# Gated convolution layer: three of four pairs of projection tiles computed by seven half-size products

## The chip, the cores and the metric

One core of a Trainium2 chip runs the kernel. The time is the device time of one execution in microseconds (us). TensorE (PE in the profile) multiplies matrices and has a row of its own for weight loads (PEld); VectorE (DVE), ScalarE (ACT) and GpSimd (POOL) work on tiles in the on-chip memory SBUF; the first two also read PSUM, where TensorE writes its sums. SyncE (SP) issues the transfers. Each engine has a queue of its own, filled in the order of the program.

## The reference

One inference step of a 4-layer decoder trunk on 512 prompt positions and 8 samples, 520 columns in all, with a model width of 1024. The layers have different mixers (matrix memory, short gated convolution, dilated attention, pooling). The change is in the second, the convolution:

```
u = h @ w_in                                  # 520x1024 @ 1024x8192
bg, cg, xb, z = split(u, 4)                   # each 2048 wide
cx = cg * xb
y  = w0 * cx[t-2] + w1 * cx[t-1] + w2 * cx[t] # three taps, per channel
out = (bg * y * silu(z)) @ w_out              # 2048x1024
```

Here h is rms_norm(x) times a gain. Everything is float32.

## The kernel before, in words

Activations lie transposed, 128 channels on the partitions and 520 columns. A float32 product is made of three products of a reduced format (float32r): each operand is split into a high part (a copy to float32r by ScalarE) and a low part (operand minus high part, by VectorE), and high x high, high x low and low x high are added up in PSUM. `mm6` (lines 193 to 203) does this for one 128x128 block of weights and all 520 columns: six matmuls, of 256 and 264 columns by turns. `proj` (213 to 225) makes one output tile of 128 channels from eight such blocks, 48 matmuls, into one of two PSUM buffers, and after every second block lets background streams take a step (`tick`).

The convolution (`conv`, 782 to 819) runs over 16 tiles of 128 channels. For tile j it projects xb, cg, bg and z (weight tiles 32+j, 16+j, j and 48+j of `w_b`), multiplies cg by xb (line 799), applies the taps (ScalarE line 807, VectorE lines 810 to 813), multiplies by bg (814) and by silu(z), and splits the result y into high and low part for the output projection (`gated`, 516 to 533).

The order of work is written out by hand. `plan` lists all weight tiles in the order of use. `weights` (181) keeps three weight tiles ahead split by `cast` (169: ScalarE line 175, VectorE line 177) and more ahead loaded by `fetch` (161), on SyncE's queue. At the start of a layer `finish_norm` (300 to 342) finishes the norm of the input behind the first projections: the mean square by a matmul (line 313), square root, reciprocal (316), then, one block of channels after the other, the normalised input (329) and its high and low parts (330, 333). Until that is done the projections use the raw input, and VectorE multiplies what comes out of PSUM by the reciprocal (`scaled`, 266 to 283). The output projection makes its first two tiles together (`proj_pair`, 227 to 241) and asks for y blocks as it needs them (`need`, 243 to 248).

Of the kernel before, what the change touches and what calls it, by code (L numbers as in the profile page):

```python
# [8 lines left out]
F32 = mybir.dt.float32  # L9
F32R = mybir.dt.float32r  # L10
# [25 lines left out]
NCOL = 120  # L36


def plan():

    out = []

    def end(i, name, halves, begun=False):
        cs = range(2 if halves else 1)
        out.extend((name, j, c) if halves else (name, j) for c in cs for j in range(2) if c or not begun)
        out.extend((name, j, c) if halves else (name, j) for j in range(2, KD) for c in cs)
        for j in range(KD):
            if j % 4 == 0:
                out.append(("w_pe", i, j // 4))
            out.append(("w_pg", i, j))  # L50

    for hd in range(H):
        out.extend(("w_a", j) for j in (hd, 8 + hd, 16 + 2 * hd, 17 + 2 * hd, 32 + 2 * hd, 33 + 2 * hd))
    out.extend(("w_a", 48 + j) for j in range(16))
    end(0, "w_ao", True)
    for j in range(16):
        out.extend(("w_b", 16 * q + j) for q in (2, 1, 0, 3))
    end(1, "w_bo", True)
    for hd in range(H):
        out.extend(("w_c", 8 * q + hd) for q in range(9))  # L60
    out.extend(("w_c", 72 + j) for j in range(H))
    end(2, "w_co", False)
    for g in range(4):
        for n, (u, i) in enumerate(POOLED):
            if g and n == 2:
                out.extend(("w_grp", g - 1, i) for i in range(2))
            out.append(("w_d", 16 * u + 4 * g + i))
    out.extend(("w_do", j, 0) for j in range(2))
    out.extend(("w_grp", 3, i) for i in range(2))
    end(3, "w_do", True, True)  # L70
    return out


class Stream:
# [39 lines left out]
class Net:  # L114
    def __init__(self, ctx, tc, d):
        self.tc, self.nc, self.d = tc, tc.nc, d
        nc = self.nc
        ctx.enter_context(tc.manual_schedule())
        pool = lambda name, **kw: ctx.enter_context(tc.tile_pool(name=name, **kw))
        self.cp = pool("const", bufs=1)  # L120
        self.wp = pool("w", bufs=3)
# [7 lines left out]
        self.gate, self.finish = Gate(0.5), None  # L129
        self.wkeys, self.wf, self.wc = plan(), {}, {}  # L130
        self.wpos = self.ndma = self.ncast = 0
# [26 lines left out]
        return self.cols[:, i : i + 1]  # L158


    def fetch(self, upto):
        while self.ndma < min(upto, len(self.wkeys)):
            key = self.wkeys[self.ndma]
            wf = self.wp.tile([P, 1024], F32, tag="wf", name=self.nm("wf"))
            self.nc.sync.dma_start(wf, self.d[key[0]][key[1:]])
            self.wf[self.ndma] = wf
            self.ndma += 1

    def cast(self, upto):
        nc = self.nc  # L170
        while self.ncast < min(upto, len(self.wkeys)):
            self.fetch(self.ncast + 1)
            wf = self.wf.pop(self.ncast)
            wh = self.wp.tile([P, 1024], F32R, tag="wh", name=self.nm("wh"), bufs=4)
            nc.scalar.activation(wh, wf, AF.Copy)  # L175
            wl = self.wp.tile([P, 1024], F32R, tag="wl", name=self.nm("wl"), bufs=4)
            nc.vector.tensor_sub(wl, wf, wh.bitcast(F32))  # L177
            self.wc[self.ncast] = (wh, wl)
            self.ncast += 1

    def weights(self, *key, ahead=4):
        i = self.wpos
        assert self.wkeys[i] == key, (self.wkeys[i], key)
        self.wpos += 1
        self.cast(i + ahead)
        self.fetch(i + 2 + ahead)
        return self.wc.pop(i)

    def tick(self):
        for s in self.streams:  # L190
# [2 lines left out]
    def mm6(self, ps, w, c, a, start, stop, m=P):  # L193

        mm = self.nc.tensor.matmul
        wh, wl = w[0][:, c : c + m], w[1][:, c : c + m]
        out = [self.part(ps, j, m) for j in range(2)]
        for j in range(2):
            mm(out[j], wh, a[0][:, PARTS[j]], start=start, stop=False)  # L199
        for j in range(2):  # L200
            mm(out[j], wh, a[1][:, PARTS[j]], start=False, stop=False)  # L201
        for j in range(2):
            mm(out[j], wl, a[0][:, PARTS[j]], start=False, stop=stop)  # L203

    @staticmethod
    def part(ps, j, m=P):
# [6 lines left out]
    def proj(self, name, *idx, a):  # L213

        ps = self.psum()
        n = len(a)
        if a is self.h:
            self.raw, a = self.hraw, list(a)
        for c in range(0, n, 8):
            w = self.weights(name, *idx, *([c // 8] if n > 8 else []))  # L220
            for k in range(8):
                self.mm6(ps, w, k * P, a[c + k], c + k == 0, c + k == n - 1)
                if k % 2:
                    self.tick()
        return ps[:, BASE : BASE + T]

    def proj_pair(self, name, a, n):

        ps = self.psum(), self.psum()
        for c in range(0, n, 8):  # L230
            w = []
            for lo, hi in ((0, 7), (7, 8)) if c + 8 == n else ((0, 8),):
                for j in range(2):
                    if not lo:
                        w.append(self.weights(name, j, *([c // 8] if n > 8 else []), ahead=4 - j))
# [6 lines left out]

    def need(self, a, i):

        while len(a) <= i:
            if not (self.gate.gens or self.gate.run):
                self.finish()
            self.gate.step()
# [51 lines left out]
    def finish_norm(self, hs, g0, wait, idle, pace):  # L300

        nc = self.nc
        self.r = self.act()
# [3 lines left out]
        def work():  # L307
# [13 lines left out]
                return  # L321
            for _ in range(idle):
                yield
            new = []
            for k in range(KD):
                for _ in range(pace):
# [14 lines left out]
        self.norm = Stream(1)  # L341
        self.norm.gens.append(work())


    def out_proj(self, name, y, i, begun=None):

# [6 lines left out]
        for j in range(KD):  # L353
# [4 lines left out]
            ps = pair[j] if j < 2 else self.proj(name, j, a=y)  # L358
            nc.vector.tensor_add(self.x[j], ps, self.x[j])  # L359
            xs.append(self.split(self.x[j]))  # L360
        return xs

    def embed(self, i, xs):
# [4 lines left out]
        for j in range(KD):  # L368
# [19 lines left out]
        self.finish_norm(hs, g0, 3, *((4, 4), (2, 3), (0, 0))[i])  # L388
        return hs

    def final(self, xs, pe, xg):
# [390 lines left out]
    def conv(self, h, lay):  # L782
        nc, d, tc = self.nc, self.d, self.tc
        self.streams = [self.norm, self.gate]
        y = []
        ex = lay.enter_context(tc.tile_pool(name="cvy", bufs=16))
        with ExitStack() as st:
            mp = st.enter_context(tc.tile_pool(name="cv", bufs=1))
            sin = mp.tile([P, 16, 2, NS], F32, name="cv_in")
# [4 lines left out]
            for j in range(16):  # L794
# [8 lines left out]
                nc.gpsimd.tensor_copy(po[:, j], cx[:, NP - 2 : NP])  # L803
                nc.gpsimd.tensor_copy(so[:, j, 1], cx[:, NP:T])
                w0, w1, w2 = (self.col(C_CW + 16 * t + j) for t in range(3))
                yc = self.act()
                nc.scalar.activation(yc, cx, AF.Copy, scale=w2)
                ps = self.proj("w_b", j, a=h)
                stt = nc.vector.scalar_tensor_tensor
                stt(yc[:, 1:NP], cx[:, 0 : NP - 1], w1, yc[:, 1:NP], ALU.mult, ALU.add)  # L810
                stt(yc[:, 2:NP], cx[:, 0 : NP - 2], w0, yc[:, 2:NP], ALU.mult, ALU.add)
                stt(yc[:, NP:T], sin[:, j, 1], w1, yc[:, NP:T], ALU.mult, ALU.add)
                stt(yc[:, NP:T], sin[:, j, 0], w0, yc[:, NP:T], ALU.mult, ALU.add)
                nc.vector.tensor_mul(yc, self.ready(ps), yc)
                z = self.scaled(self.proj("w_b", 48 + j, a=h), func=AF.Silu)
                self.gated(y, z, yc, True, pools=(None, ex))
            nc.sync.dma_start(d["o_conv_p"], po)
            nc.sync.dma_start(d["o_conv_s"], so)
        return y
# [519 lines left out]
```

## Time and profile before

| | us |
|---|---|
| median of 3 runs (1 core) | 2192.27 |
| lowest and highest run | 2191.33 and 2192.53 |
| the profiled execution, its own time | 2191.75 |
| its span, first to last instruction | 2190.0 |
| TensorE busy in the span | 2170.4 (99%) |
| mean granted TensorE clock | 0.999 of full speed |

The page of the profile gives the busy time of each engine, the chain of work that ended last (followed back from the last instruction), and groups of instructions by line and shape. The trace behind it can be asked for a stretch, a line or the order of time. A matmul's shown duration contains its way through the array, which overlaps the next one, so the pace of matmuls is read from the distance of their starts or from counts over a stretch.

### The profile page before, as it was taken

How to read it: one execution, taken by the hardware profiler on the slowest of the kernel's cores; microseconds unless marked ns; L12 is line 12 of the kernel's file. 1: busy time of each engine (PE TensorE's matmuls, PEld its weight loads, DVE VectorE, ACT ScalarE, POOL GpSimd, SP SyncE). 2: the span in 40 equal slices, each digit the busy share in tenths (PEclk: the TensorE clock that was granted, in tenths of full speed). 3: DMA queues.
4: the chain of work that ended last, by engine and by line, in shares of the span. 5: the costliest groups of instructions: out<-in, count | busy, mean ns of one | idle time of the engine just before them, and what ended most of it. 6: DMA issues, size and time to landing. Idle time of an engine off the chain costs nothing.

```text
span 2190.0 us, 42581 instructions
## 1 busy us (share of the span) xinstructions
PE 2170.4 (99%) x17788; PEld 2154.2 (98%) x17788; DVE 1336.6 (61%) x2984; ACT 784.0 (36%) x1286; POOL 226.8 (10%) x338
## 2 busy tenths in 40 slices
PE   9999999999999999999999999999999999999998
PEld 8999999999999999999999999999999999999998
DVE  7677676653575344333467877787777466676434
ACT  6444444432442222222333323333335343222233
POOL 1101110100000000000014232232220000000000
PEclk9999999999999999999999999999999999999999
DMA  4643544333232322233233645554545233323421
GB/s 151 203 163 139 184 168 150 98 97 97 90 97 87 97 89 95 92 105 95 83 103 127 187 168 179 172 181 155 184 161 194 87 106 97 97 88 97 124 88 51
DMA packets 104643, 275.17 MB, mean 126 GB/s; under 512 B 33316, under 2 KB 37668, under 8 KB 102404
## 3 DMA queue, kind: packets, MB, share of 16 engines
q1 hardware_dynamic: 104308, 272.41, 38.3%
q8 instruction: 139, 2.28, 0.4%
q14 instruction: 52, 0.43, 0.1%
q10 hardware_dynamic: 144, 0.06, 0.0%
HBM read 249.61 MB, written 22.82 MB: 124 GB/s over the span
## 4 chain that ended last, share of the span: by engine, by line
PE 91%; DVE 3%; ACT 1%; POOL 1%; issue 0%; DMA 0%; SPq 0%; POOLq 0%; DVEq 0%; ACTq 0%
PE ps L199 27%; PE ps L201 27%; PE ps L203 27%; PE ax L925 1%; PE ax L998 1%; PE ax L201 1%; PE ax L203 1%; PE ax L199 1%; PE ax L969 1%; PE ax L654 1%; PE ax L673 1%; DVE wl L177 1%; DVE a L329 0%; POOL a L877 0%; PE ax L936 0%
## 5 line engine op out<-in xcount | busy, mean ns | idle before, releaser
L199 PE MATMUL ps<-hi,wh 128*128 128x256 f32 (+1 forms) x5280 | 1086.3, 287 | 2.1 <-DVE a L278 1.6
L201 PE MATMUL ps<-lo,wh 128*128 128x256 f32 (+1 forms) x5280 | 1062.9, 283 | 0.1
L203 PE MATMUL ps<-hi,wl 128*128 128x256 f32 (+1 forms) x5280 | 1063.1, 283 | 0.0
L199 PEld LDWEIGHTS ps<-hi,wh 128*128 128x128 f32 x5280 | 822.3, 189 | 7.6 <-issue 2.5
L201 PEld LDWEIGHTS ps<-lo,wh 128*128 128x128 f32 x5280 | 819.3, 188 | 0.3 <-DVE lo L530 0.3
L203 PEld LDWEIGHTS ps<-hi,wl 128*128 128x128 f32 x5280 | 818.3, 188 | 0.0
L177 DVE TENSOR_TENSOR wl<-wf,wh 128x1024 fp32r<-128x1024 f32 x344 | 429.2, 1249 | 397.1 <-ACT wh L175 395.5
L175 ACT ACTIVATE wh<-wf 128x1024 fp32r<-128x1024 f32 x344 | 361.0, 1051 | 253.2 <-issue 201.7
L271 ACT ACTIVATE a<-ps 128x520 f32<-128x520 f32 x94 | 56.3, 599 | 247.7 <-PE ps L203 243.5
L876 POOL TENSOR_TENSOR a<-a,a 32x520 f32<-32x520 f32 x48 | 74.0, 1542 | 386.2 <-DVE a L278 199.6
L359 DVE TENSOR_TENSOR x<-ps,x 128x520 f32<-128x520 f32 x32 | 22.4, 699 | 103.4 <-PE ps L203 103.3
L278 DVE TENSOR_TENSOR a<-ps,a 128x520 f32<-128x520 f32 x95 | 65.9, 694 | 25.9 <-PE ps L203 22.5
L282 ACT ACTIVATE a<-a 128x520 f32<-128x520 f32 x43 | 27.5, 639 | 150.2 <-DVE a L278 150.0
L259 ACT ACTIVATE hi<-x 128x520 fp32r<-128x520 f32 x32 | 20.5, 639 | 164.6 <-DVE x L359 164.6
L877 POOL TENSOR_TENSOR a<-a,a 32x520 f32<-32x520 f32 x48 | 66.4, 1384 | 124.8 <-DVE a L875 88.7
L902 ACT ACTIVATE S<-S,nmx 128x128 f32<-128x128 f32 (+1 forms) x96 | 40.0, 417 | 76.1 <-DVE nmx L899 76.1
L252 DVE CUSTOM_DVE_ANT_0 kc<-kc,qb 128x128 f32<-128x128 f32 (+1 forms) x192 | 56.8, 350 | 12.5 <-DMA kc<-kc 12.5
L252 DVE CUSTOM_DVE_ANT_0 vc<-vc,pb 128x128 f32<-128x128 f32 (+1 forms) x192 | 61.6, 379 | 0.0
L880 DVE TENSOR_TENSOR a<-a,a 32x520 f32<-32x520 f32 x48 | 37.2, 776 | 17.3 <-POOL a L877 17.3
L260 DVE TENSOR_TENSOR lo<-a,hi 128x520 fp32r<-128x520 f32 x40 | 28.0, 699 | 31.3 <-ACT hi L259 31.3
L732 DVE SCALAR_TENSOR_TENSOR Ci<-kqb,wv,Ci 128x128 f32<-128x128 f32 x128 | 37.1, 346 | 12.2 <-DMA kqb<-scr_kq 10.1
L528 ACT ACTIVATE hi<-a 128x520 fp32r<-128x520 f32 x40 | 25.4, 635 | 50.6 <-DVE a L525 50.6
(272 smaller groups left out, 1759.7 us busy)
## 6 DMA issues: line engine op xcount, KB each, us to landing
wf<-w_c SPq DMA_DIRECT2D x80, 512.0 KB
wf<-w_a SPq DMA_DIRECT2D x64, 512.0 KB
wf<-w_b SPq DMA_DIRECT2D x64, 512.0 KB
wf<-w_pg SPq DMA_DIRECT2D x32, 512.0 KB
wf<-w_d SPq DMA_DIRECT2D x32, 512.0 KB
pb<-scr_p SPq DMA_DIRECT2D x8, 1292.0 KB
Ci<-C_in SPq DMA_DIRECT2D x16, 512.0 KB
kqb<-scr_kq SPq DMA_DIRECT2D x8, 1024.0 KB
```

The lines of the kernel that those rows point to most:

```text
L175: nc.scalar.activation(wh, wf, AF.Copy)
L177: nc.vector.tensor_sub(wl, wf, wh.bitcast(F32))
L199: mm(out[j], wh, a[0][:, PARTS[j]], start=start, stop=False)
L201: mm(out[j], wh, a[1][:, PARTS[j]], start=False, stop=False)
L203: mm(out[j], wl, a[0][:, PARTS[j]], start=False, stop=stop)
L252: self.nc.vector.tensor_tensor_reduce(junk, a, b, 1.0, 0.0, ALU.mult, ALU.add, out)
L271: nc.scalar.activation(dst[:, :T], ps, func, scale=scale)
L278: nc.vector.tensor_mul(dst[:, :T], ps, self.r)
L876: nc.gpsimd.tensor_mul(b[:32], t[:32], cs[0])
L877: nc.gpsimd.tensor_mul(a[:32], a[:32], cs[1])
L880: nc.vector.tensor_add(t[:32], a[:32], b[:32])
L902: nc.scalar.activation(blk, blk, AF.Exp, bias=nmx[:, i : i + 1], scale=SCALE, accum_out=l[:, i : i + 1])
```

## The change

**Seven products.** Two weight tiles (W1, W2: two output tiles) form one item of the plan. Each is cut into two halves of 512 input channels, the 520 columns into two halves of 260. That is a 2x2 by 2x2 product of blocks, which Winograd's form of Strassen's method makes with seven block products instead of eight, and with sums before and after. `seven` does it; a product is four blocks of 128 channels with three matmuls of 260 columns each. Three weight sums (s1, s2, s4) and the difference that replaces half of W2 are made by GpSimd; ScalarE and VectorE split them. Partial products r1 and r6 have PSUM banks of their own and are written on to after they were read; r4 and r5 share a buffer of two banks. The last product of a pair is held back (`pend`) and runs within the next pair, after its second product, or in the middle of the next projection.

**Which tiles.** Tiles 0 and 1 stay plain. From tile 2 on (xb, cg) are always a pair; (bg, z) are one in even tiles, while in odd tiles they stay two plain projections.

**The input.** Right behind the norm, `summed` makes the normalised input block by block, and four half-width differences for each pair of blocks on GpSimd, with their high and low parts (T1 to T4). All of it is finished before tile 2 (`norm.drain()`).

**The order.** `due` simulates the plan with an assumed cost for each item (5.76 us a projection, 10.08 a pair) and gives each load, sum and split a due time, as its buffers come free; `pump` issues what is due as the matmuls go by (0.72 us for each `mm6`, 1.44 for each product). For a pair that begins at t the sums are due at t - 14.1, high and low parts between t - 14.4 and t - 0.8, both later where a buffer is not free yet. SBUF has four buffers each for loaded, high and low weights (three for loaded ones before), and four more for the parts of the sums. The scratch space for DMAs is cut to 1024.

**Behind the stage.** The products y are split into high and low parts when the output projection begins (`parts`), four blocks ahead of use (`look`); its first two tiles now go block by block together.

The core of the diff:

```diff
+def paired(j):
+    return 0 if j < NPLAIN else 2 - j % 2
...
+            one = at(max(ld, ld2, t - 14.1), i, "sum")
+            h1 = at(max(ld, take("wh", t + 5.76), t - 14.4), i, "high")
+            h2 = at(max(ld2, take("wh", t + 10.08), one + 4), i, "high2")
+            low1 = at(max(h1 + 1.3, one + 3), i, "low")
+            low2 = at(max(h2 + 1.3, one + 3), i, "low2")
...
+            for n, need, until in (("2", t - 7.2, t + 2.88), ("1", t - 5.7, t + 8.64), ("4", t - 1.4, t + 14.4)):
+                h = at(max(take("hs", until), need, one + 3), i, "high" + "s" + n)
+                at(h + 0.6, i, "lows" + n)
...
+        elif op == "sum":
+            w1, w2 = t["w1"], t["w2"]
+            s1, s2, s4 = (self.act()[:, :512] for _ in range(3))
+            nc.gpsimd.tensor_add(s1, w2[:, a], w2[:, b])
+            sub(w2[:, a], w1[:, a], w2[:, a])
+            sub(s2, s1, w1[:, a])
+            sub(s4, w1[:, b], s2)
...
+    def seven(self, keys, B, dst, done):
...
+        def product(out, w, name, start):
+            for k in range(4):
+                c = slice(k * P, (k + 1) * P)
+                hi, lo = B[name][k]
+                go = {} if start else {"skip_group_check": True}
+                mm(out, w[0][:, c], hi, start=start and k == 0, stop=False, **go)
+                mm(out, w[0][:, c], lo, start=False, stop=False, **go)
+                mm(out, w[1][:, c], hi, start=False, stop=k == 3, **go)
...
+        def last():
+            product(r5, part("s4"), "22", False)
+            add(dst[0][:, HALF:], r5, u2)
+            done()
+            step()
+
+        product(r1, part("1", a), "11", True)
+        nc.scalar.activation(s1, r1, AF.Copy)
+        step()
+        product(r6, part("s2"), "T2", True)
+        add(u2, r6, s1)
+        step()
+        self.flush()
+        product(r1, part("1", b), "21", False)
+        nc.scalar.activation(dst[0][:, :HALF], r1, AF.Copy)
+        step()
+        product(r6, part("2", a), "T3", False)
+        add(u3, r6, s1)
+        step()
+        product(r5, part("s1"), "T1", True)
+        step()
+        product(r4, part("2", b), "T4", True)
+        pair = lambda x, n: x.rearrange("p (u c) -> p u c", u=2)[:, :, :n]
+        add(pair(dst[1], HALF), pair(v, HALF), u3.unsqueeze(1).broadcast_to([P, 2, HALF]))
+        step()
+        self.pend = last
...
+        for k in range(4):
+            t, u = self.act(), self.act()
+            for dst, j in ((t, k), (u, k + 4)):
+                nc.vector.scalar_tensor_tensor(dst, self.x[j], self.col(g0 + j), r, ALU.mult, ALU.mult)
+            yield
+            ta, tb = self.act(), self.act()
+            sub(ta[:, a], t[:, b], t[:, a])
+            sub(tb[:, a], u[:, b], t[:, b])
+            sub(ta[:, b], u[:, b], ta[:, a])
+            sub(tb[:, b], u[:, a], ta[:, b])
...
+            for h, l, x in zip(hs, ls, (ta, tb)):
+                nc.vector.tensor_sub(l, x, f(h))
...
+                self.seven((("w_b", 32 + j), ("w_b", 16 + j)), self.sums, (xb, cx), first)
...
+                if paired(j) > 1:
+                    self.seven((("w_b", j), ("w_b", 48 + j)), self.sums, (bg, z), second)
+                else:
+                    ps = self.proj("w_b", j, a=h)
+                    nc.vector.tensor_mul(c[0], ps, c[0])
+                    ps = self.proj("w_b", 48 + j, a=h)
```

`first` multiplies cg by xb and applies the taps; `second` takes the silu of z and multiplies by bg; `times` multiplies both together.

## Rows read from the trace of the kernel before

**Rows 1.** The page: span and busy time of each engine (share of the span, instructions).

```profile
span 2190.0 us, 42581 instructions
...
PE 2170.4 (99%) x17788; PEld 2154.2 (98%) x17788; DVE 1336.6 (61%) x2984; ACT 784.0 (36%) x1286; POOL 226.8 (10%) x338
```

**Rows 2.** The page: the chain that ended last, share of the span by engine.

```profile
PE 91%; DVE 3%; ACT 1%; POOL 1%; issue 0%; DMA 0%; SPq 0%; POOLq 0%; DVEq 0%; ACTq 0%
```

**Rows 3.** Stretches: us, busy PE, PEld, DVE, ACT, POOL (instructions), clock, DMA share, GB/s.

```profile
602.60:648.40 45.80, 45.80 (x380) 45.68 (x379) 32.80 (x45) 18.26 (x23) 0.86 (x5) 1.00 0.30 93
...
740.00:786.00 46.00, 46.00 (x386) 46.00 (x386) 18.60 (x24) 12.97 (x16) 0.62 (x4) 1.00 0.30 93
```

**Rows 4.** Line 810, first tap: count, duration min/median/max in ns, first and last start.

```profile
L810 DVE SCALAR_TENSOR_TENSOR a<-a,cols,a x16: 743/745/748, 620.2 to 963.9; 128x511 f32<-128x511 f32 x16
```

**Rows 5.** The chain in order of time: start us, us; last output tile.

```profile
2167.77 4.26 PE ps L410 x36
```

**Rows 6.** VectorE in order of time, start of the convolution: start us, us, line, operands.

```profile
619.50 0.76 DVE L329 SCALAR_TENSOR_TENSOR a<-x,cols,a 128x520 f32<-128x520 f32 x1
620.17 0.75 DVE L810 SCALAR_TENSOR_TENSOR a<-a,cols,a 128x511 f32<-128x511 f32 x1
620.96 0.75 DVE L811 SCALAR_TENSOR_TENSOR a<-a,cols,a 128x510 f32<-128x510 f32 x1
621.62 0.22 DVE L812 SCALAR_TENSOR_TENSOR a<-cv_in,cols,a 128x8 f32<-128x8 f32 x1
...
622.02 0.69 DVE L278 TENSOR_TENSOR a<-ps,a 128x520 f32<-128x520 f32 x1
...
632.31 0.69 DVE L525 TENSOR_TENSOR a<-a,a 128x520 f32<-128x520 f32 x1
632.92 0.69 DVE L278 TENSOR_TENSOR a<-ps,a 128x520 f32<-128x520 f32 x1
634.66 1.23 DVE L177 TENSOR_TENSOR wl<-wf,wh 128x1024 fp32r<-128x1024 f32 x1 [1.04 <-ACT wh L175]
635.80 0.75 DVE L329 SCALAR_TENSOR_TENSOR a<-x,cols,a 128x520 f32<-128x520 f32 x1
```

**Rows 7.** Groups by line and shape, whole span: busy us, mean ns, idle before.

```profile
L177 DVE TENSOR_TENSOR wl<-wf,wh 128x1024 fp32r<-128x1024 f32 x344 | 429.2, 1249 | 397.1 <-ACT wh L175 395.5
...
L380 DVE TENSOR_TENSOR a<-ax,a 128x264 f32<-128x264 f32 x31 | 13.1, 423 | 0.0
...
L175 ACT ACTIVATE wh<-wf 128x1024 fp32r<-128x1024 f32 x344 | 361.0, 1051 | 253.2 <-issue 201.7 <-PE ps L201 39.3 <-DMA wf<-w_c 5.2
```

**Rows 8.** GpSimd: line 628, a tiny operation; then VectorE and GpSimd in attention.

```profile
L628 POOL TENSOR_TENSOR a<-a,a x8: 1273/1292/1409, 73.6 to 354.6; 128x512 f32<-128x512 f32 x8
...
L1093 POOL TENSOR_TENSOR vn<-vn,pb 128x24 f32<-128x24 f32 x8 | 2.2, 269 | 44.3 <-DMA pb<-scr_p 44.3
...
1145.58 0.74 DVE L329 SCALAR_TENSOR_TENSOR a<-x,cols,a 128x520 f32<-128x520 f32 x1
...
1148.25 1.22 DVE L177 TENSOR_TENSOR wl<-wf,wh 128x1024 fp32r<-128x1024 f32 x1
1149.38 1.80 DVE L329 SCALAR_TENSOR_TENSOR a<-x,cols,a 128x520 f32<-128x520 f32 x1
...
1148.48 2.15 POOL L876 TENSOR_TENSOR a<-a,a 32x520 f32<-32x520 f32 x1 [5.29 <-DVE a L278]
```

**Rows 9.** Start of the convolution in order of time: ScalarE, TensorE, VectorE.

```profile
602.84 0.61 ACT L378 ACTIVATE a<-ps 128x520 f32<-128x520 f32 x1 [1.40 <-PE ps L203]
...
608.36 1.04 PE L313 MATMUL ax<-a,onesd 128*128 128x256 f32 x4
609.04 0.60 PE L199 MATMUL ps<-hi,wh 128*128 128x256 f32 x2
...
609.50 3.42 DVE L316 RECIPROCAL a<-a 128x256 f32<-128x256 f32 x2 [1.02 <-ACT a L314]
```

More of the change, by code (lines that the diff above doesn't have):

```diff
@@ L65, in plan, with due, take, at @@
             if g and n == 2:
[L66 to L69, printed above, removed]
+                for m in range(2):
+                    add("w_grp", g - 1, m)
+            add("w_d", 16 * u + 4 * g + i)
+    for j in range(2):
+        add("w_do", j, 0)
+    for m in range(2):
+        add("w_grp", 3, m)
     end(3, "w_do", True, True)
     return out
+def due(items):
+    ops, t, seq = [], 0.0, 0
+    slots = {"wf": [0.0] * FBUFS, "wh": [0.0] * HBUFS, "hs": [0.0] * SBUFS}
+    def take(tag, until):
+        free = slots[tag]
+        at = min(free)
+        free.remove(at)
+        free.append(until)
+        return at
+    def at(time, i, op):
+        nonlocal seq
+        ops.append((time, seq, i, op))
+        seq += 1
+        return time
+    for i, it in enumerate(items):
+        it.begin = t
+        if len(it.keys) == 1:
+            ld = min(slots["wf"])
+            sp = at(max(ld, take("wh", t + (it.life or it.cost))), i, "split")
+            at(take("wf", sp) - 0.01, i, "load")
+        else:
+            ld, ld2 = sorted(slots["wf"])[:2]
+            one = at(max(ld, ld2, t - 14.1), i, "sum")
[3 more added lines that the diff above has]
+            low2 = at(max(h2 + 1.3, one + 3), i, "low2")
+            at(take("wf", max(low1, one + 5.8)) - 0.01, i, "load")
+            at(take("wf", low2) - 0.01, i, "load2")
+            for n, need, until in (("2", t - 7.2, t + 2.88), ("1", t - 5.7, t + 8.64), ("4", t - 1.4, t + 14.4)):
+                h = at(max(take("hs", until), need, one + 3), i, "high" + "s" + n)
+                at(h + 0.6, i, "lows" + n)
+        t += it.cost
+    return sorted(ops)
 class Stream:
@@ L128, in __init__ @@
         self.streams = []
-        self.gate, self.finish = Gate(0.5), None
-        self.wkeys, self.wf, self.wc = plan(), {}, {}
-        self.wpos = self.ndma = self.ncast = 0
+        self.gate, self.finish, self.look = Gate(0.5), None, 0
+        self.items = plan()
+        self.ops, self.begun, self.made = due(self.items), 0, set()
+        self.wt, self.wpos, self.clock, self.pend = {}, 0, 0.0, None
         self.cols = self.cp.tile([P, NCOL], F32, name="cols")
@@ new lines, in pump @@
+    def pump(self, step=0.0):
+        nxt = self.items[min(self.wpos, len(self.items) - 1)].begin
+        self.clock = max(self.clock, min(self.clock + step, nxt))
+        while self.begun < len(self.ops) and self.ops[self.begun][0] <= self.clock + 0.01:
+            self.make(*self.ops[self.begun][2:])
+            self.begun += 1
+    def fetch(self, upto):
+        for i in range(upto):
+            self.make(i, "load")
+    def cast(self, upto):
+        for i in range(upto):
+            self.make(i, "load")
+            self.make(i, "split")
@@ L182, in weights, with item @@
+    def item(self, *keys):
         i = self.wpos
-        assert self.wkeys[i] == key, (self.wkeys[i], key)
+        assert self.items[i].keys == keys, (self.items[i].keys, keys)
         self.wpos += 1
-        self.cast(i + ahead)
-        self.fetch(i + 2 + ahead)
-        return self.wc.pop(i)
+        self.clock = self.items[i].begin
+        self.pump()
+        while any((j, op) not in self.made for _, _, j, op in self.ops[self.begun :] if j == i):
+            self.make(*self.ops[self.begun][2:])
+            self.begun += 1
+        return self.wt.pop(i)
@@ L189, in tick, with weights @@
+    def weights(self, *key):
+        t = self.item(key)
+        return t["h1"], t["l1"]
     def tick(self):
@@ L234, in proj_pair @@
                     if not lo:
-                        w.append(self.weights(name, j, *([c // 8] if n > 8 else []), ahead=4 - j))
+                        w.append(self.weights(name, j, *([c // 8] if n > 8 else [])))
+                    if c == 0 and self.look:
+                        if j:
+                            for k in range(8):
+                                self.need(a, k)
+                                for m in range(2):
+                                    self.mm6(ps[m], w[m], k * P, a[k], k == 0, False)
+                                self.tick()
+                        continue
                     for k in range(lo, hi):
@@ L298, in square_in, with finish_norm @@
             nc.vector.tensor_add(self.acc, self.acc, sq)
-    def finish_norm(self, hs, g0, wait, idle, pace):
+    def finish_norm(self, hs, g0, wait, idle, pace, sums=None):
         nc = self.nc
@@ L323, in work @@
                 yield
+            if sums is not None:
+                hs[:] = yield from self.summed(g0, r, sums)
+                self.hraw = False
+                return
             new = []
@@ L360, in out_proj @@
             xs.append(self.split(self.x[j]))
+        self.look = 0
         return xs
@@ L387, in embed @@
             self.square_in(j)
-        self.finish_norm(hs, g0, 3, *((4, 4), (2, 3), (0, 0))[i])
+        self.sums = {} if i == 0 else None
+        self.finish_norm(hs, g0, 3, *((4, 1), (2, 3), (0, 0))[i], sums=self.sums)
         return hs
@@ new lines, in parts @@
+            def parts(n):
+                hi = self.act(F32R, "hi", ex if n > 3 else None)
+                nc.scalar.activation(hi, yf[n], AF.Copy)
+                yield
+                lo = self.act(F32R, "lo")
+                nc.vector.tensor_sub(lo, yf[n], hi.bitcast(F32))
+                y.append((hi, lo))
+            for j in range(NPLAIN, 16):
+                block(j)
+            self.flush()
+            self.gate.drain()
+            while self.gate.run:
+                self.gate.step()
@@ L817, in conv @@
+            self.gate.gens.extend(parts(n) for n in range(4, 16))
+            self.look = 4
             nc.sync.dma_start(d["o_conv_p"], po)
```

203 lines of the change are left out of this document (159 added, 44 removed).

## The prediction

> **What bounds the kernel now.** The busy shares come first: TensorE is busy 99% of the 2190.0 us span, VectorE 61%, ScalarE 36%, GpSimd 10% [rows 1]. A busy TensorE alone proves little, so the chain that ended last is read next: it runs 91% through matmuls and 3% through VectorE [rows 2]. Then the changed stage by itself: in a steady 46 us of the convolution TensorE has no gap, VectorE works 18.6 us, ScalarE 13.0, GpSimd 0.6; in its first 45.8 us VectorE already works 32.8 [rows 3]. So the time of this stage is its matmuls times their pace, with a cover of 27 us in 46 on VectorE later on, and of 13 in 46 at the start.
>
> **The pace of a matmul.** One tile (four projections of 48 matmuls) repeats every (963.9 - 620.2)/15 = 22.91 us [rows 4], so a matmul of 260 columns on average takes 22.91/192 = 0.1193 us. In the old order two matmuls in a row share their weights and write different columns; the new products change weights every one or two matmuls and write one region twelve times running. The nearest row is the last output tile, which keeps one half of the columns through all its matmuls: 36 in 4.26 us, 0.118 each [rows 5]. I take 0.1193 for the new ones.
>
> **What is removed.** A pair of projections costs 96 matmuls. Seven products of 4 blocks and 3 matmuls cost 84. Tiles 2 to 15 have seven even ones with two pairs each and seven odd ones with one, 21 pairs: 21 x 12 x 0.1193 = 30.1 us less on TensorE. An even tile falls from 22.9 to 168 x 0.1193 = 20.0 us, an odd one to 180 x 0.1193 = 21.5; both together from 45.8 to 41.5.
>
> **What is added to VectorE.** Its durations overlap slightly when it runs without gaps, so the distance of starts is the price: 0.61 us for a 520-column operation, 0.67 to 0.79 for a three-operand one, 0.40 for two tiny ones, 1.14 for a 1024-column low part [rows 6, 7]. A pair needs two low parts (2.28), three half-width ones (scaled from 0.61: 3 x 0.60), three 260-column additions out of PSUM (3 x 0.42, [rows 7]) and one of 520 (0.61): 5.95 us. The convolution itself needs 3.7 us a tile (three products 1.83, taps 0.79 + 0.66 + 0.40). Even tile: 2 x 5.95 + 3.7 = 15.6 of 20.0 us. Odd tile: 5.95 + two plain low parts 2.28 + 3.7 = 11.9 of 21.5. ScalarE's two full high parts (2 x 1.05, [rows 7]), three halves and two copies come to under 5 us a pair; it stays hidden.
>
> **What is added to GpSimd, and what that takes from VectorE.** Each pair's weight sums are four chained 512-column operations; such a one takes 1.29 us [rows 8], so 5.2 us in a pair of 10.0. GpSimd has the time, but it isn't free: in the attention stage a three-operand VectorE operation takes 0.74 us with GpSimd quiet and 1.80 when it is issued just after a GpSimd operation got in, and that GpSimd operation in turn takes 2.15 instead of 1.29, having waited for the low part before it [rows 8]. The two engines take turns, at a price of 1.80 - 0.74 = 1.06 us of VectorE for one GpSimd operation. Twelve in an even and an odd tile cost 12.7 us; with VectorE's own 27.5 that is 40.2 of 41.5 us, before anything waits for anything. Additions out of PSUM are 6.2 of it and may run under GpSimd.
>
> The Trainium skill, SBUF — State Buffer, section "Who interferes with whom", states this rule: a VectorE instruction with two SBUF inputs and a GpSimd instruction that reads SBUF exclude each other for a whole instruction. The trace agrees on the exclusion and shows less than the whole. With 1.29 instead of 1.06 the two tiles would need 43.0 us, above TensorE's 41.5, a loss of 1.5 x 7 = 10 us in place of the stalls below. The row decides here.
>
> **Where TensorE waits, steady state.** Weight preparation is due some 8 us or more before use and absorbs delay. The evictions don't: the partial sum in the second product's bank must be read before the fourth product writes on there. In the second pair of an even tile three low parts (1.14 + 0.60 + 1.14) stand ahead of that read in VectorE's queue, with about two and a half GpSimd operations between them (2.65); with the read (0.42) and 0.9 for the addition that ends the first pair this is 6.9 us, and TensorE comes to the fourth product after four products, 48 x 0.1193 = 5.7. It waits some 1.1 us, seven times: 7.7 us. From below the price is 0, if the order leaves GpSimd in VectorE's idle gaps. From above an even tile must hold all of its own load, 15.6 + 8 x 1.06 = 24.1 for 20.0: 4.1 x 7 = 29 us. I take 7.7, since odd tiles have 21.5 - 11.9 - 4.2 = 5.4 us to spare and take on most of it: the sums of an even tile's first pair lie in the odd tile before.
>
> **The start of the stage.** The first product needs the whole normalised input, and the second all its differences. Both are now made during tiles 0 and 1 alone, instead of three. From the end of the reciprocals at 612.9 to the end of the eighth projection (602.8 + 45.8 + 0.7 for the norm's own matmuls = 649.3) lie 36.4 us [rows 9]. VectorE's own work there: eight normalising operations 5.4, sixteen low parts 9.8, thirteen products 7.9, taps 3.7, four plain low parts 4.6, the first pairs' 5.2: 36.7, already full. GpSimd adds sixteen half-width differences (by the 24- and 512-column rows about 0.76 each, hence some 0.53 of hindrance: 8.5) and about seven sum operations (7.4), of which at most 4.9 can lie under reads of PSUM: 11 to 16 us. Used from the second product's last block on, 2.5 us into the pair, the last low part is late by 36.7 + 11 - 36.4 - 2.5 = 9 us, at worst 13.5. Without any hindrance it would be 0. I take 9, as the rows show the hindrance. If so long a gap also lowers TensorE's clock, which is at full speed through the stage before [rows 3], the next matmuls cost up to double; that I leave to the range.
>
> **Smaller edits.** The products' high and low parts move behind the stage into the output projection: 0.61 us on VectorE for each y against 12 matmuls, 1.43 us, of cover per y; without cover the first would cost 2 us, I take 0.5. The planner moves weight loads and splits in all other stages; they stay three projections ahead, bytes are the same, and I take 0 between -2 and +2. The smaller DMA scratch costs nothing on the path: it has no instruction there.
>
> **Sum.** The profiled execution took 2191.75 us (span 2190.0 and 1.75 around it), 0.5 below the median of 2192.27. 2191.75 - 30.1 + 7.7 + 9 + 0.5 = 2178.9, say 2179. About 0.2% (4.4 us) is what a measurement here tells from no change.
>
> **Rivals.**
> - *The cover holds.* VectorE's gaps take GpSimd's work, the start costs 0 to 4, the steady state next to nothing: 2162 to 2169. For it: 40.2 is below 41.5, and loads and splits are due early. Against it: the full start. Chance 0.24.
> - *VectorE and GpSimd become the bound, slower.* One queue serves evictions and weight parts, so a late queue holds TensorE. From a stall of (4.4 + 30.1 - 9.5)/7 = 3.6 us in each even tile the kernel is slower than before; at 4.1, with 13.5 at the start and 2 at each of the small terms, 2208. For it: 24.1 against 20.0 in an even tile. Against it: the odd tile's 5.4 to spare. Chance 0.13.
> - *The new matmuls are slower.* No gain is left if each of the 1764 takes 0.1364 us, even without a stall; with 0.14 the sum is 2198 with no stall and 2215 with mine. The row at 0.118 speaks against it. Chance 0.05.
> - *The gain is used up.* Start near 13 and stalls of 1.7 to 2.9 us: 2187 to 2196. Chance 0.15.
>
> **How the numbers follow.** My forecast, 2179 with its own range from 2170 (start 4, stalls 0.5) to 2187 (start 12, stalls 2), has 0.43. Faster by over 0.2%: 0.43 + 0.24 = 0.67. Within: 0.15. Slower: 0.13 + 0.05 = 0.18. The range reaches from 2163 to 2196, leaving out most of the slower cases and the rest of the first rival.
>
> **What would show it.** 1764 matmuls in the products, 0.119 us apart inside one. GpSimd busy some 120 us more (84 x 1.29 + 16 x 0.76), at elongated means. VectorE's low parts in the stage with a mean well above 1.25 [rows 7]. A TensorE gap of about 9 us around the first pair, ahead of the second product, released by VectorE's low part, and gaps of about 1 us ahead of fourth products, released by the addition. No gap at either place makes the first rival right; gaps of over 3 us in every even tile the second. A gap ahead of matmuls that wait for weights, not for an eviction, would make my steady-state reasoning wrong whatever the total.

## The result and the profile after

The changed kernel takes 2282.16 us in the median of four runs (2281.20 to 2291.68) against 2191.80 before: 1.042 times the time, 95% interval 1.039 to 1.045. It is 90 us slower, where 13 us faster was forecast; the range ended at 2196. The profiled execution is the slowest of the four, 2291.68 us, so its stretches are some 9 us longer in all than the median's.

First the page: span, busy time, TensorE's granted clock in 40 slices, and the chain that ended last.

```profile
span 2289.5 us, 42551 instructions
...
PE 2183.1 (95%) x17536; PEld 2155.5 (94%) x17536; DVE 1498.3 (65%) x3134; ACT 835.5 (36%) x1387; POOL 376.1 (16%) x438
...
PEclk9999999999998989989999999999999999999999
...
PE 43%; DVE 5%; issue 3%; ACT 3%; POOL 1%; DMA 0%; ACTq 0%; POOLq 0%; SPq 0%; DVEq 0%
```

Against [rows 1] and [rows 2]: TensorE lost its share, 95% of a longer span instead of 99%, and the chain runs through it for 43% instead of 91%. New in the clock row are three slices, the 13th, 15th and 18th, below nine tenths of full speed; the mean granted clock fell from 0.999 to 0.981. Between the outputs x of the four output projections (the first addition to the first block of x in each layer) the time went like this:

| first x of the | before, us | after, us | longer by, in this stretch |
|---|---|---|---|
| first layer | 475.07 | 493.84 | 18.8 |
| second (convolution) | 994.13 | 1075.75 | 62.9 |
| third | 1700.41 | 1792.70 | 10.7 |
| end of the span | 2190.0 | 2289.5 | 7.2 |

The convolution, from which 30.1 us of matmuls were taken, became 62.9 us longer, and the other layers, whose matmuls are the same, 36.7. Whom TensorE waited for, in the whole span (us in total, times, longest), the first five and one further down:

```profile
PE ax L353 <- DVE a L371: 22.0, 7, 3.5
PE ps L353 <- DVE a L384: 15.9, 6, 3.2
PE ps L325 <- DVE x L605: 13.3, 4, 3.3
PE ps L325 <- DVE a L476: 9.4, 12, 1.9
PE ax L353 <- ACT hi L567: 7.9, 1, 7.9
...
PE ps L327 <- DVE lo L1114: 3.0, 1, 3.0
```

Lines 371 and 384 are the additions by which VectorE takes partial products out of PSUM in `seven`; 605 is the addition to x at an output projection; 476 takes a raw projection out of PSUM; 567 makes high parts of the normalised input; 1114 makes low parts of y at the output projection. The first four wait for an eviction, the last two for parts of activations, and none of the six for weights. Now stretches, with the columns of [rows 3]: tiles 0 and 1, the start of the pairs, one even and one odd tile, and two short ones around a gap.

```profile
622.00:668.00 46.00, 43.69 (x358) 43.04 (x358) 38.43 (x44) 20.30 (x27) 21.25 (x20) 1.00 0.25 84
668.00:710.00 42.00, 29.07 (x189) 27.66 (x188) 34.34 (x40) 16.79 (x28) 20.79 (x18) 0.76 0.23 76
710.00:762.00 52.00, 47.40 (x378) 46.78 (x377) 41.77 (x44) 19.63 (x30) 24.79 (x20) 0.97 0.24 82
843.00:847.00 4.00, 0.68 (x6) 0.47 (x4) 4.00 (x3) 1.85 (x3) 2.67 (x2) 0.90 0.44 131
847.00:851.00 4.00, 3.78 (x17) 3.78 (x18) 2.15 (x5) 0.00 (x0) 0.00 (x0) 0.50 0.42 131
```

Before, a steady 46 us held 386 matmuls at full clock [rows 3]; here 52 us hold 378, VectorE shows 41.8 us busy and GpSimd 24.8. The last two lines show the clock: TensorE did 0.68 us of work in the first four microseconds, and in the next four it is granted 0.50 of full speed (its 1.2 GHz level), so that they hold 17 matmuls. Not every gap had this: after the gap of 3.20 us that ended at 765.85 the granted clock of the next four microseconds was 1.00.

What makes the gap is seen in a stretch like it. GpSimd's timeline (start us, us; in brackets the idle time ahead and what ended it) just ahead of one:

```profile
778.86 0.18 POOL L1045 COPY cv_p<-a 128x2 f32<-128x2 f32 x1 [15.29 <-DVE a L1087]
...
779.12 1.29 POOL L269 TENSOR_TENSOR a<-wf 128x512 f32<-128x512 f32 x1
780.50 1.63 POOL L270 TENSOR_TENSOR wf<-wf,wf 128x512 f32<-128x512 f32 x1
782.09 1.74 POOL L271 TENSOR_TENSOR a<-a,wf 128x512 f32<-128x512 f32 x1
783.90 1.31 POOL L272 TENSOR_TENSOR a<-wf,a 128x512 f32<-128x512 f32 x1
785.17 1.82 POOL L269 TENSOR_TENSOR a<-wf 128x512 f32<-128x512 f32 x1
787.07 1.63 POOL L270 TENSOR_TENSOR wf<-wf,wf 128x512 f32<-128x512 f32 x1
788.66 2.27 POOL L271 TENSOR_TENSOR a<-a,wf 128x512 f32<-128x512 f32 x1
791.01 1.59 POOL L272 TENSOR_TENSOR a<-wf,a 128x512 f32<-128x512 f32 x1
```

VectorE's timeline of the same kernel and stretch:

```profile
783.89 1.34 DVE L1057 SCALAR_TENSOR_TENSOR a<-cv_in,cols,a 128x8 f32<-128x8 f32 x1
785.15 0.68 DVE L254 TENSOR_TENSOR ls<-a,hs 128x512 fp32r<-128x512 f32 x1
785.76 0.68 DVE L1104 TENSOR_TENSOR a<-ps,a 128x520 f32<-128x520 f32 x1
786.37 1.17 DVE L254 TENSOR_TENSOR ls<-a,hs 128x512 fp32r<-128x512 f32 x1
787.46 2.32 DVE L254 TENSOR_TENSOR wl<-wf,wh 128x1024 fp32r<-128x1024 f32 x1
789.70 1.77 DVE L254 TENSOR_TENSOR ls<-a,hs 128x512 fp32r<-128x512 f32 x1
791.40 2.29 DVE L254 TENSOR_TENSOR wl<-wf,wh 128x1024 fp32r<-128x1024 f32 x1
793.61 0.41 DVE L371 TENSOR_TENSOR a<-ax,a 128x260 f32<-128x260 f32 x1
```

The eight GpSimd operations are the sums of two pairs, one behind the other. Ahead of them in GpSimd's queue stand two small copies for the taps, and GpSimd was idle for 15.29 us until VectorE's product of the odd tile (line 1087) let the first of them go; both pairs' sums came right behind. VectorE's operations between 783.9 and 793.6 alternate with them: the tap on 8 columns takes 1.34 us instead of 0.22, a low part of 1024 columns 2.3 instead of 1.22, one of 512 columns 1.77 instead of 0.68. The eviction that TensorE waits for (line 371) comes at 793.61, and TensorE stood from 790.5 to 794.1. `ls` at 785.15 and the read of PSUM at 785.76 have their plain durations. VectorE isn't idle in these 9.7 us, so the eviction doesn't come late because a low part waits for a sum: the seven operations ahead of it are longer, and at plain durations they would add up to 5.4 us.

The groups of the steady stretch from 700 to 1040 us say it in means (busy us, mean ns | idle before):

```profile
L254 DVE TENSOR_TENSOR wl<-wf,wh 128x1024 fp32r<-128x1024 f32 x55 | 87.0, 1591 | 2.0 <-ACT wh L250 2.0
L254 DVE TENSOR_TENSOR ls<-a,hs 128x512 fp32r<-128x512 f32 x58 | 56.2, 978 | 0.0
...
L1057 DVE SCALAR_TENSOR_TENSOR a<-cv_in,cols,a 128x8 f32<-128x8 f32 x14 | 14.2, 1016 | 0.5
L1056 DVE SCALAR_TENSOR_TENSOR a<-cv_in,cols,a 128x8 f32<-128x8 f32 x14 | 13.5, 966 | 0.0
```

In other layers the loss has another form. Below is the timeline at the first output projection after the change, in order of time:

```profile
490.46 2.00 ACT L250 ACTIVATE wh<-wf 128x1024 fp32r<-128x1024 f32 x2 [9.72 <-PE ps L327]
...
491.56 2.36 DVE L254 TENSOR_TENSOR wl<-wf,wh 128x1024 fp32r<-128x1024 f32 x2 [9.56 <-ACT wh L250]
...
493.84 0.69 DVE L605 TENSOR_TENSOR x<-ps,x 128x520 f32<-128x520 f32 x1
```

VectorE's timeline of the kernel before at the same place:

```profile
475.07 0.70 DVE L359 TENSOR_TENSOR x<-ps,x 128x520 f32<-128x520 f32 x1 [8.67 <-PE ps L203]
...
479.45 2.36 DVE L177 TENSOR_TENSOR wl<-wf,wh 128x1024 fp32r<-128x1024 f32 x2 [0.26 <-ACT wh L175]
```

Before, the addition to x started at 475.07, as TensorE ended, and the low parts of the next weights came behind it. Now two high parts that waited for TensorE to leave their buffers (9.72 us) and two low parts stand ahead of the addition, and TensorE, which needs that PSUM buffer, stood for 3.34 us. In the profile this is one gap in each of the four layers (13.3 us); the same order stands in all plain projections. In the whole span the idle time ahead of ScalarE's high parts of weights (line 250) that ended with TensorE's line 327 is 319.0 us, against 39.3 us for line 201 before. That the second PSUM buffer hides most of it from TensorE was not tested.

### The profile page after: what moved, and what is told of

Same layout as the page of the kernel before. It is cut to its first block, busy times and chain, and to the rows that moved or that the text cites. A ratio compares the mean times of both kernels' runs of the same rounds, so it can differ in the third digit from the quotient of the medians.

```text
span 2289.5 us, 42551 instructions
## 1 busy us (share of the span) xinstructions
PE 2183.1 (95%) x17536; PEld 2155.5 (94%) x17536; DVE 1498.3 (65%) x3134; ACT 835.5 (36%) x1387; POOL 376.1 (16%) x438
## 4 chain that ended last, share of the span: by engine, by line
PE 43%; DVE 5%; issue 3%; ACT 3%; POOL 1%; DMA 0%; ACTq 0%; POOLq 0%; SPq 0%; DVEq 0%
PE ps L325 12%; PE ps L327 12%; PE ps L329 12%; PE ax L1306 1%; ACT S L1210 1%; PE ax L325 1%; ACT wh L250 1%; PE ax L327 1%; PE ax L329 1%; PE ax L1233 1%; DVE a L1188 1%; DVE kc L450 1%; DVE wl L254 1%; PE ax L1277 1%; POOL a L1185 0%
## 5 line engine op out<-in xcount | busy, mean ns | idle before, releaser
L325 PE MATMUL ps<-hi,wh 128*128 128x256 f32 (+1 forms) x4608 | 953.5, 288 | 30.8 <-DVE x L605 13.3
L327 PE MATMUL ps<-lo,wh 128*128 128x256 f32 (+1 forms) x4608 | 929.2, 283 | 3.3 <-DVE lo L1114 3.0
L329 PE MATMUL ps<-hi,wl 128*128 128x256 f32 (+1 forms) x4608 | 928.9, 283 | 0.2 <-DVE wl L254 0.2
L325 PEld LDWEIGHTS ps<-hi,wh 128*128 128x128 f32 x4608 | 719.2, 189 | 40.1 <-issue 23.7
L327 PEld LDWEIGHTS ps<-lo,wh 128*128 128x128 f32 x4608 | 715.9, 189 | 3.7 <-DVE lo L1114 3.2
L329 PEld LDWEIGHTS ps<-hi,wl 128*128 128x128 f32 x4608 | 716.3, 189 | 0.5 <-DVE wl L254 0.5
L250 ACT ACTIVATE wh<-wf 128x1024 fp32r<-128x1024 f32 x344 | 361.4, 1054 | 570.7 <-PE ps L327 319.0
L627 DVE TENSOR_TENSOR a<-ax,a 128x256 f32<-128x256 f32 (+1 forms) x62 | 23.7, 423 | 71.0 <-ACT a L625 71.0
L254 DVE TENSOR_TENSOR ls<-a,hs 128x512 fp32r<-128x512 f32 x63 | 61.2, 980 | 0.0
L250 ACT ACTIVATE hs<-a 128x512 fp32r<-128x512 f32 x63 | 38.6, 623 | 54.7 <-issue 39.2
L353 PE MATMUL ax<-hi,wh 128*128 128x260 f32 x168 | 49.7, 296 | 7.9 <-ACT hi L567 7.9
```

The lines of the kernel that those rows point to most:

```text
L250: nc.scalar.activation(t["h" + k], t["w" + k], AF.Copy)
L254: nc.vector.tensor_sub(t["l" + k], t["w" + k], f(t["h" + k]))
L353: mm(out, w[0][:, c], hi, start=start and k == 0, stop=False, **go)
```

## The experiments

Three causes were put to the test, A: the order of weight splits and evictions; B: turns between GpSimd and VectorE at SBUF; C: VectorE's amount of work at the start and in pairs. A fourth, D, loads in SyncE's queue, came up on the way. The kernel before ran at 2191.6 to 2193.2 us beside them.

**A: the split behind the eviction.** `pump` reaches the next item's begin during the last `mm6` of a projection, so that a split that is due then is issued ahead of the eviction. With a margin it is issued by the next item:

```diff
-        nxt = self.items[min(self.wpos, len(self.items) - 1)].begin
+        nxt = self.items[min(self.wpos, len(self.items) - 1)].begin - (0.05 if step else 0)
```

> Theory A (order): in the changed kernel a weight split that waits for TensorE to leave its buffer is issued ahead of the eviction of the projection that just ended, so ScalarE (1.05 us) and VectorE (1.23 us) come to the eviction late in every layer. Issued behind the eviction, the first layer's first output x should come at 475 to 478 us instead of 493.8, the gaps of 3.3 us at the four output projections should go, and the time should fall from 2282 to about 2242; the gaps of 3.5 and 3.2 us in the convolution stay. Rival: the split is needed that early, and gaps ahead of matmuls that wait for weights take their place: under 10 us of gain.

2240.65 us: 41.5 less. The gaps at the output projections are gone, those of 0.7 and 3.0 us for the late parts of y with them, and the two in the steady convolution stay, in TensorE's waits of this run, the first of them as it was:

```profile
PE ax L353 <- DVE a L371: 21.9, 7, 3.6
PE ps L353 <- DVE a L384: 11.4, 6, 3.2
```

The first x came at 483.93, not at 475 to 478: half of the first layer's loss has another cause. Much of the gain lies in the convolution itself: between the profiled executions 24.3 us, 557.6 from first x to first x instead of 581.9.

**B: no sums.** The four GpSimd operations of `sum` are left out; the products take unsummed halves in their place:

```diff
-            s1, s2, s4 = (self.act()[:, :512] for _ in range(3))
-            nc.gpsimd.tensor_add(s1, w2[:, a], w2[:, b])
-            sub(w2[:, a], w1[:, a], w2[:, a])
-            sub(s2, s1, w1[:, a])
-            sub(s4, w1[:, b], s2)
-            t.update(ws1=s1, ws2=s2, ws4=s4)
+            t.update(ws1=w2[:, a], ws2=w1[:, a], ws4=w1[:, b])
```

> Leaves out the weight sums on GpSimd: the products take unsummed halves of the loaded weights in their place, VectorE's and ScalarE's work is the same. Theory B (turns at SBUF): VectorE's delay in the steady convolution is GpSimd's four sum operations a pair, each taking a turn before a VectorE operation. Then two tiles fall from about 52 us to 41.5 to 43, the gaps of 3.5 and 3.2 us go and with them the lowered clock: 2282 to about 2215. Rival: VectorE's own queue, in which weight parts stand ahead of the evictions, is late without GpSimd too: the gaps stay above 2 us and the gain is under 25 us.

2221.93 us: 60 less, and from 681 us, inside the first pair, to the output projection no gap over 0.3 us is left. VectorE's low parts have their plain durations again, in the groups of the stretch from 700 to 960 us of this run:

```profile
L254 DVE TENSOR_TENSOR wl<-wf,wh 128x1024 fp32r<-128x1024 f32 x51 | 61.7, 1220 | 14.1 <-ACT wh L250 14.1
L254 DVE TENSOR_TENSOR ls<-wf,hs 128x512 fp32r<-128x512 f32 x55 | 37.1, 684 | 0.0
```

So the number of VectorE's operations is not what made the evictions late: the same ones, 371 ns shorter for each low part of 1024 columns (1591 less 1220) and 294 for each of 512, leave no gap.

**B: the sums on VectorE.** `tensor_add` and `tensor_sub` of `sum` and `summed` on VectorE instead of GpSimd:

```diff
-        sub = nc.gpsimd.tensor_sub
+        sub = nc.vector.tensor_sub
...
-            nc.gpsimd.tensor_add(s1, w2[:, a], w2[:, b])
+            nc.vector.tensor_add(s1, w2[:, a], w2[:, b])
...
-        sub = nc.gpsimd.tensor_sub
+        sub = nc.vector.tensor_sub
```

> Weight sums and input differences on VectorE instead of GpSimd. Theory B: a sum costs VectorE 0.6 us itself against a turn of 1.06 us and more given to GpSimd, so VectorE gets faster though it does more: gaps in the convolution at most 2 us, 2282 to between 2225 and 2250. Rival: VectorE's amount of work is what counts, and 2.4 us more in each pair of 10 us makes it slower than 2282.

2222.06 us, 60 less and a little better than expected: doing the sums costs VectorE no more, in the end, than leaving them out. The stretch of an even and an odd tile, with the columns of [rows 3]:

```profile
740.00:782.00 42.00, 42.00 (x353) 42.00 (x352) 35.03 (x56) 17.86 (x27) 0.62 (x4) 1.00 0.31 99
```

353 matmuls in 42.00 us without a gap: 0.1190 us each. VectorE does all that it did, and the sums of three pairs on top, in 35.0 us; in the changed kernel it took 41.8 in 52 without the sums.

**A and B together.**

> Splits behind evictions and sums on VectorE. Theories A and B together: the gains add up, 2190 to 2212, near the kernel before. If this is well below 2192, the seven products pay once both causes are gone; if it stays above 2225, a third cause is at work.

2187.05 us, 0.998 times the kernel before (0.997 to 0.999). The gains nearly add up: 41.5 and 60.1 one by one, 95.1 together. The steady part is now as forecast for the case without stalls; what is left lies at the start of the pairs, in the first of these two stretches:

```profile
646.00:690.00 44.00, 33.08 (x238) 31.50 (x238) 37.91 (x62) 17.97 (x30) 1.56 (x4) 0.84 0.23 72
...
774.00:816.00 42.00, 42.00 (x353) 42.00 (x353) 36.32 (x58) 18.10 (x28) 0.62 (x4) 1.00 0.31 101
```

Between the first x of the first two layers it takes 506.5 us; 519.06 before, less 30.1, would be 489.0. So 17.5 us are lost in the start: gaps of 3.7, 4.2 and 1.4 us, some smaller ones, and a mean clock of 0.84 in 44 us.

**C: the normalised input four steps earlier**, by `(0, 1)` for `(4, 1)` in `embed`'s call of `finish_norm`.

> As the kernel with both changes (2187), but the normalised input is begun four steps, 5.7 us, earlier. Theory C: at the start VectorE's amount of work in tiles 0 and 1 is what delays the first pair; begun earlier it still has the same work: the gaps of 11.6 us fall by less than 3, 2183 to 2187. Rival: the chain of steps is too long, then the start comes 5 us or more earlier: 2179 to 2182.

2189.49 us and gaps of 12.1: no gain, even 2 us more, which lie in the first layer (first x at 483.71 instead of 481.13); the convolution takes 506.1 us instead of 506.5. So the chain of steps isn't what holds the start up.

**C: three plain tiles**, `NPLAIN = 3`.

> As the kernel with both changes (2187), but tiles 0 to 2 are plain. Theory C: 22.9 us more of cover at the start take away its gaps and the lowered clock, some 17 us, for 2.9 us of matmuls: 2171 to 2177, below the kernel before by 15 to 21. Rival: the gap moves to the first pair wherever it is: 2185 to 2192.

2179.92 us, 0.994 (0.993 to 0.996): some 7 less, but 3 above the expected 2171 to 2177. The gaps around the first pair are gone; the convolution takes 496.7 us where 27.2 us less of matmuls (19 pairs) would make 491.9. The first x came at 483.76, so the remaining loss is in the first layer.

**D: later loads.** Loads for single tiles are due 5.75 us later, where they were due over 11.6 us ahead of the split:

```diff
-            at(take("wf", sp) - 0.01, i, "load")
+            ld = take("wf", sp) - 0.01
+            at(ld + 5.75 if sp - ld > 11.6 else ld, i, "load")
```

> As the kernel with three plain tiles (2180), but each weight load is issued one projection later, as before the change, when the buffer it goes into is already free. Theory D: the first layer is still 6 to 12 us longer because a load that waits for its buffer stands in SyncE's queue ahead of the state's loads and stores; then the first x comes back from about 484 to 475 to 478 us and the time to 2170 to 2175. Rival: the loads aren't the cause, 2177 to 2183 and the first x at 481 or later.

2171.71 us, 0.991 (0.989 to 0.992), with the first x at 474.29, where it was before the change. The waits of SyncE's queue in the first 480 us (line that waits, for what, us in total, times, longest), of the kernel before, of the one with three plain tiles, and of this one:

```profile
SPq L165 <- DVE wl L177: 137.8, 31, 8.8
...
SPq L720 <- DMA scr_kq<-kqt: 11.6, 8, 5.4
```

```profile
SPq L262 <- DVE wl L254: 216.2, 41, 8.8
...
SPq L968 <- DMA scr_kq<-kqt: 37.5, 8, 5.5
```

```profile
SPq L263 <- DVE wl L255: 153.2, 35, 13.9
...
SPq L969 <- DMA scr_kq<-kqt: 12.5, 8, 5.8
```

A load that waits for the low part that still reads its buffer holds up what stands behind it in SyncE's queue; the transfer of k and q to all partitions, for one, waits 37.5 us for its source instead of 11.6. With fewer such waits both are nearly back.

**C: two pairs in every tile**, `return 0 if j < NPLAIN else 2` in `paired`, on top of it.

> As the one before, but with two pairs in every tile from the third on: 6 or 7 more pairs, 9 us less on TensorE. Theory C: VectorE, with the sums on it, then has 20.4 us of work in tiles of 20.0 and holds TensorE up: no gain, 2172 to 2190, gaps ahead of matmuls released by VectorE. Rival: it still fits, 2162 to 2167.

2179.69 us: 8 slower with 10.0 us less of matmuls (seven pairs of 1.43). TensorE's waits of this run:

```profile
PE ps L354 <- DVE a L385: 11.5, 13, 1.5
```

It waits 13 times for the last addition of a pair (line 385 here, 384 in the changed kernel). In a stretch of two tiles VectorE has 37.9 us of work in 40:

```profile
740.00:780.00 40.00, 38.27 (x313) 37.45 (x312) 37.92 (x60) 18.64 (x31) 0.62 (x4) 1.00 0.33 102
```

In this order of work three of four pairs is what VectorE can serve, once it makes the sums itself.

**A, in the kernel before.** `self.cast(self.wpos + 4)` at the end of `proj` and of `proj_pair`, ahead of the eviction, with nothing else changed:

> The kernel before with one thing of the change alone: the weight split that waits for the buffer of the projection just issued is put ahead of that projection's eviction, with no pairs and no planner. Theory A: this order by itself costs the 40 us that its removal gave back, spread over all layers: 2222 to 2237, the first x at 485 to 495 us instead of 475, gaps of 3.3 us at the output projections. Rival: the order only hurts together with the planner's loads; then below 2202.

2278.22 us, 86 more, far beyond the expected 2222 to 2237. The first layer lost only 6 us (first x at 481.02); the surprise is a gap that the changed kernel doesn't have, at the gates of the embeddings, as TensorE's waits of this run show:

```profile
PE ax L199 <- DVE a L383: 38.8, 14, 3.3
PE ps L199 <- DVE x L362: 13.3, 4, 3.3
```

There a split stands ahead of the sigmoid of each block. So this run shows that the order alone, without pairs and planner, costs tens of us and makes the same 13.3 us of gaps at the output projections; its total isn't the share of the order in the change.

**No pairs at all**, `NPLAIN = 16` with A's margin, GpSimd still making the differences of the input, and all of y split late.

> Splits behind evictions, and no pairs at all: sixteen plain tiles under the planner, with its norm and its late splitting of y. It measures what planner and norm cost without the seven products. The first layer was still 6 us longer than before with splits behind evictions, so 2196 to 2202; rival: everything but the pairs is free, 2190 to 2193.

2213.45 us, above the expected 2196 to 2202. The first layer had lost 12.5 us (first x at 487.57) and the convolution 9.2. The kernels with A's margin and the early loads have the same program up to there, and their first x comes between 481.1 and 487.6, so this part isn't steady from kernel to kernel; with later loads it was 474.3 and 475.9. Of the convolution's 9.2 us the gaps show 5.0 and a clock of 0.88 in the 14 us from 986 some 1.7. The rest is pace: 766 matmuls in 92.00 us without a gap from 700 on, 0.1201 us each, against 386 in 46.00 before, 0.1192; why is not shown.

## Why the prediction was wrong

**The step "I take 0 between -2 and +2" for the planner** is the first that failed. The weights do stay three projections ahead and the bytes are the same, as it said. But a due time that falls on the end of a projection puts a split, with a wait for TensorE and 2.3 us of ScalarE and VectorE, ahead of the eviction. Moved behind it, the kernel gained 41.5 us. In the kernel with three plain tiles another 8 us (2179.9 to 2171.7) lay in loads that wait in SyncE's queue. The working counted instructions and lead, and didn't ask what is queued behind the moved ones: both SyncE's queue and the evictions.

**The step "Where TensorE waits, steady state"** is the second, and by its size the larger: 1.1 us for an even and an odd tile, at most 4.1. The gaps were 3.5 and 3.2 us, and the lowered clock made the period 52.1 us (gaps at 740.05 and 1000.64, five periods apart) where 41.5 was computed: 10.6 us in each of these five periods, 53 us, and one more gap of 3.53 us with its lowered clock behind them, where 7.7 was put for all seven even tiles (the first had gaps of 0.87 and 1.03). The mechanism was named, the place only half: one gap is ahead of the fourth product of an even tile's *first* pair, the other at the held-back product of its second. The price of a turn was about right, 1.06 us against 2.32 - 1.22 and 1.77 - 0.68, and so was the load, 40.2 us for VectorE in two tiles against 41.8 in the 52 us shown. Three things about it were wrong. First, the eight operations of two pairs were spread over time by their due times; nothing holds GpSimd's queue to those, and it ran them one behind the other into the same 14 us, behind a copy that had waited 15.29 us for VectorE. Second, two and a half turns were put ahead of the eviction, on the low parts; the taps take turns too, 1.0 us in the mean instead of 0.22 on 8 columns, and the operations from 783.89 on were 4.3 us longer in all than at plain durations. Third, the clock was left to the range; there it could widen it by a few us, but in every period it costs 4 (52.1 less 41.5 and 6.7).

**The rival "VectorE and GpSimd become the bound"** was the right one in kind, with 0.13 and at most 2208. Its bound, 24.1 us of load in an even tile, counted durations and no waiting: with evictions, splits and TensorE in one loop, VectorE was busy or blocked for 41.8 us of 52 and idle for the rest, waiting for TensorE. A sum of loads near 97% of the period was read as "fits"; with two engines that wait for each other it didn't.

**The rule of the Trainium skill** (SBUF — State Buffer, "Who interferes with whom") that VectorE, with two inputs in SBUF, and GpSimd, reading SBUF, exclude each other for a whole instruction was set aside for the row, 1.06 against 1.29, for 10 us. The trace after agrees with the exclusion, at 1.1 us a turn; neither figure gave the size, since the waits behind it decide. The same page, in "Summary: rules for kernel authors", advises to schedule whichever of the two is off the critical path; the run with the sums on VectorE went further and took GpSimd out, for 60 us.

**The start** was right in kind: 9 us of gap, at worst 13.5, and 13 were measured around the first pair; the mean clock of 0.76 in 42 us, only mentioned, cost some 6 more (42 less 12.9 of gaps and less 189 matmuls at 0.119). The place was wrong: the largest gap, 7.9 us, is ahead of the last block of the first product and ends with ScalarE's high part of the normalised input; only 3.0 and 0.6 us lie at the second product's last block, where the forecast had all of it. With GpSimd's sums left out and its sixteen differences still in place, gaps of 1.7, 0.7 and 4.2 us stayed there, so the sums' hindrance was about half of it. VectorE's amount of work as the cause fits the runs, since more cover removed the gaps and an earlier beginning didn't.

**The late splitting of y**, put at 0.5 us, made two gaps of 0.7 and 3.0 us in the changed kernel; with the splits behind the evictions both are gone, so they go with the first step.

**Right** were the pace of the matmuls (0.119), the 30.1 us of matmuls (the fastest version: 19 pairs, 27.2 us of matmuls, 21 us of time), and the signs by which to tell: gaps of over 3 us released by the addition were the second rival's mark.

## What to carry to other kernels

When a helper engine is given work beside another that shares a path to memory with it, count turns, not microseconds, small instructions included, and look whether the busy engine could do the work itself for less. A planner's due time orders a queue and nothing more: ask of every moved instruction what it waits for and which eviction or transfer stands behind it, first at the boundary between two tiles. With these two mended the kernel was level with the one before (2187.05 us against 2191.64); with a third plain tile and later loads, seven products for eight matmul blocks did pay: 2171.7 us against 2193.2.

## What the runs showed of the hardware

An instruction on 8 columns with two SBUF operands took 0.97 to 1.02 us in the mean beside a busy GpSimd, 0.22 without it, while reads of PSUM kept their durations beside it (0.70 us at 520 columns, 0.42 at 260). After the gap of 3.5 us that ended at 847.2 TensorE was granted 0.50, its 1.2 GHz level, in the next four microseconds; after one of 3.2 us it kept 1.00. In the mean of the five periods a gap cost about half as much again as it shows: 6.7 us of gaps and some 4 of lowered clock.
